# A hybrid decoder layer: the byte positions of the matmul operands in on-chip memory

## Chip, cores, metric

The kernel runs on one core of a Trainium2 chip. The metric is device time in microseconds (us), the median of several executions; lower is better. A profile of one execution comes with it, and "us" and "ns" below are read from that profile or from the times.

## The reference

One decoder layer on 1024 tokens with 16 meta tokens in front (1040 rows of 1024 features), float32. Cut to what matters:

```python
h = concatenate([meta, x])                       # (1040, 1024)
a = rmsnorm(h, ln_mix_pre)
dq, dk, dv, hq, hf, hi, hg = split(a @ w_in)     # w_in: (1024, 3584)
y_diff = diff_attention(dq, dk, dv, ...)         # 4 heads, softmax difference
y_hgrn = hgrn2(hq, hf, hi, hg, ...)              # 4 heads, gated linear recurrence
h = h + rmsnorm(concatenate([y_diff, y_hgrn]) @ w_out, ln_mix_post)
a = rmsnorm(h, ln_ffn_pre)
u = causal_conv3(a @ w_ffn_up) + conv_b          # w_ffn_up: (1024, 5632)
y = (gelu(gate_half(u)) * up_half(u)) @ w_ffn_down   # (2816, 1024)
return (h + rmsnorm(y, ln_ffn_post))[16:]
```

## The kernel before

Nearly all of the time goes into matrix products. A float32 operand is split into a rounded high part and a low part, and a product is made of three matmuls into one PSUM bank: high x high, high x low, low x high. A matmul has a *stationary* operand (128 x 128, loaded into the array by a separate weight load) and a *moving* operand (128 partitions x N columns, streamed through). Each matmul of the program has its own weight load, which the page lists as PEld.

The stages, in the order of the program:

- **Projections**, mixed with attention and recurrence by `interleave` (a generator that feeds projection matmuls between the steps of the heads). Stationary: 128 x 128 pieces of the projection weights (`wh`, `wl`). Moving: the normed activations `ahi`, `alo`, cut in three groups of columns, 272 in the first and 384 in the two others. Lines 237, 239, 241 and 889. With 28 weight tiles, 8 steps of the contraction and three matmuls each, there are 672 matmuls with 272 columns and 1344 with 384. The attention scores are lines 654 and 655.
- **Output projection** in two halves: stationary is the mixed activations (`mp`, from DRAM), moving the split weights, 512 columns. Lines 1016, 1018, 1020.
- **Up stage** of the feed-forward part. The tokens stand in two parts, p = 0 (2 x 258 columns) and p = 1 (2 x 256). For the first of the 22 pairs of feature blocks the products are plain (`plain_unit`, lines 1360 to 1362); for the other 21 each 2 x 2 block product is done with 7 products in the place of 8 (`unit`, lines 1379 to 1381, with `pa`, `pb`, `pc` as the PSUM banks). Stationary: `uh`, `ul`, made from sums of weight tiles. Moving: the activations' sums, tiles `t0_0` to `t0_7` and `t1_0` to `t1_7`, first digit p, second the product; each holds a high and a low half of 4 steps x 258 or 256 columns. They are made by `t_split` and `t_sums` through `t_tiles`, in pools that had room when they were made (`ep`, `mxp`, `tp`, `t2p`).
- **Down stage**, again 7 products in the place of 8: stationary `gh`, `gl`, moving `wh`, `wl`, 512 columns. Lines 1538 to 1540.

TensorE runs in the order in which the code is written. Tiles come from pools: a pool at the left side of the 224 KiB partition grows upwards, a pool at the right side grows downwards, and each tile's byte position follows from the sizes of those allocated before it (rounded up to 32 bytes). Nothing else sets the positions. Worked out from the sizes, as bytes past a multiple of 512: before the change the weights `wh`, `wl`, `uh`, `ul`, the down stage's operands, `mp` and all the p = 1 tiles begin at 480. The p = 0 tiles begin at 480 too, save `t0_0` (352) and `t0_4` (416); their rows are 1032 bytes long, so each of the 4 steps begins 8 bytes later, and most low halves begin 32 bytes after the high ones. `ahi` and `alo` are read at 416 (272 columns) and 480 (384 columns). Every one of the weight positions is thus 32 bytes past a multiple of 64.

Of the kernel before, what the change touches and what calls it, by code (L numbers as in the profile page):

```python
# [9 lines left out]
F32 = mybir.dt.float32  # L10
F32R = mybir.dt.float32r
# [6 lines left out]
P = 128  # L18
# [13 lines left out]
WN = [258, 256]  # L32
# [53 lines left out]
def layer_kernel(ctx: ExitStack, tc: tile.TileContext, x, meta, table, lbl, gpre, gpost, win,  # L86
# [7 lines left out]
    def pool(name, bufs, side="left", space=None):  # L94
        kw = {"side": side} if space is None else {"space": space}
        cm = tc.tile_pool(name=name, bufs=bufs, reuse_waits="tile", **kw)
        return cm, cm.__enter__()

    def close(*cms):
        for cm in cms:  # L100
            cm.__exit__(None, None, None)
# [2 lines left out]
    ctx.enter_context(tc.manual_schedule(engines={mybir.EngineType.PE}))  # L104

    c_cm, cp = pool("const", 1)
    w_cm, wp = pool("weights", 1, "right")
    d_cm, dp = pool("scratch", 1, space=bass.MemoryType.DRAM)
    p_cm, pp = pool("ps0", 1, space=PSUM)
    deep = {"ip": 3, "m": 5}  # L110

    def const(shape, name, dt=F32):
        return cp.tile(shape, dt, tag=name, name=name)
# [12 lines left out]
    nlam = const([P, 1], "nlam")  # L126
    cwt = const([P, 2 * NF, 3], "cwt")
    cbt = const([P, 2 * NF], "cbt")
    m0 = const([P, 88], "m0", F32R)[:, :46]
    G.memset(m0.bitcast(F32), 0.0)  # L130
    m0_7 = const([P, 2, 1, 2], "m0_7", F32R)

# [34 lines left out]
    mx_cm, mxp = pool("mix", 1)  # L167

    MIX = {"X0": 2048, "X1": 2176, "X2": 2176}
# [14 lines left out]
                         m[:, l, off:off + P * n].bitcast(F32).rearrange("p (b c) -> p b c", c=P))  # L184

    at_cm, atp = pool("at", 1)
    ahi, alo = (atp.tile([P, KD, P * NBLK], F32R, tag=t, name=t)[:, :, P - META:] for t in ("ahi", "alo"))

    last_load, lows = [], []
# [771 lines left out]
    p_cm, pp = pool("ps", 2, space=PSUM)  # L961
# [46 lines left out]
    def tok(i):  # L1008
        return (2, 14) if i == 0 else (P, start(i))
# [12 lines left out]
    def meta_part(py, wo, full):  # L1022
        for k in range(KD - 1):
            hi, lo = wo[k]
            both = [(34, hi), (2, lo)]
            if k == KD - 2:
                both.reverse()
            for i, (r, w) in enumerate(both):
                T.matmul(py[:r], m0[:, 2 * k:2 * k + r], w, start=(k == 0 and i == 0), stop=(r == 34 and k == KD - 2))
                yield 216  # L1030
            if k == 0 and full:
                yield from out_part(m0_7, py, wo[KD - 1:], range(1), False, False)
# [18 lines left out]
    def second_load(i):  # L1051
        blocks[i] = block_tile(1, i)
        block_load(blocks[i], i, 0, 4)
        block_load(blocks[i], i, 4, 7 if i == 1 else 8)
# [8 lines left out]
    def y0_gain(p):  # L1063
        r = tok(p)[0]
        return G.tensor_tensor(y0[:r, p], y0[:r, p], gpo0[:r], op=ALU.mult)
# [38 lines left out]
    p_cm, pp = pool("ps3", 8, space=PSUM)  # L1104

    def ps_b(name):
        return pp.tile([P, 512], F32, tag="b", name=name)


    sw_cm, swp = pool("sums", 1, "right")  # L1110
    e_cm, ep = pool("early", 1, "right")
# [74 lines left out]
    def load_xh(i):  # L1186
        r = tok(i)[0]
        if i:
            xhs[i] = qp.tile([P, D], F32, tag="xh", name=f"xh{i}")
        else:  # L1190
            xhs[i], xhs["sum"] = xh0[:, :D], xh0[:, D:]
        SY.dma_start(xhs[i][:r], meta[14:16, :] if i == 0 else x[P * (i - 1): P * i, :])
# [32 lines left out]
    def trans(i):  # L1225
        r, t0 = tok(i)
        a2 = a2t.pop(i)
        cs = slice(t0 - 14, t0 - 14 + r)
        for half in range(2):
            pt = ps_b(f"pa2_{i}_{half}")  # L1230
            for j in range(4):
                k = 4 * half + j
                T.transpose(pt[:, j * r:(j + 1) * r], a2[:r, P * k: P * (k + 1)], ident[:r, :r])
            pv = pt[:, : 4 * r].rearrange("p (k t) -> p k t", k=4)
            ks = slice(4 * half, 4 * half + 4)
            for p in range(2):
                lo_, hi_ = max(cs.start, C0[p]), min(cs.stop, C0[p] + 2 * WN[p])
                if lo_ < hi_:
                    A.copy(
                        at2[p][:, ks, lo_ - C0[p]:hi_ - C0[p]], pv[:, :, lo_ - cs.start:hi_ - cs.start])  # L1240
# [1 line left out]
    tt = [[None] * 8 for _ in range(2)]  # L1242

    def t_tiles(p, j, where, tag):
        tag, n, lo = (tag + (8 * WN[p], 4 * WN[p])[len(tag) - 1:])[:3]
        flat = where.tile([P, n], F32R, tag=tag, name=f"t{p}_{j}")
        return [flat[:, o:o + 4 * WN[p]].rearrange("p (a c) -> p a c", a=4) for o in (0, lo)]

    def t_split(p, j, src, where, *tag):
        hi, lo = t_tiles(p, j, where, tag)  # L1250
        A.copy(hi, src)
        V.tensor_tensor(lo, src, hi.bitcast(F32), op=ALU.subtract)
        tt[p][j] = (hi, lo)

    def quarter(p, j):
        n = WN[p]
        a, c = {0: (0, 0), 7: (0, n), 4: (4, 0), 6: (4, n)}[j]
        return at2[p][:, a:a + 4, c:c + n]

    def t_sums(p, where, last):  # L1260
        b11, b12, b21, b22 = (quarter(p, j) for j in (0, 7, 4, 6))
        V.tensor_tensor(b11, b12, b11, op=ALU.subtract)
        V.tensor_tensor(b12, b22, b12, op=ALU.subtract)
        V.tensor_tensor(b22, b22, b11, op=ALU.subtract)
        for j, b in ((1, b22), (2, b11), (3, b12)):
            t_split(p, j, b, where, f"t{p}_{j}", *(() if p else (2304, 1152) if j == 3 else (2176,)))
        V.tensor_tensor(b21, b21, b22, op=ALU.subtract)
        t_split(p, 5, b21, *last)

    def run(*args):  # L1270
        for _ in out_part(*args):
            pass

    def k7(i):
        return m7[:, i - 1:i].rearrange("p b l t -> p l b t")

    for i in range(1, NBLK):
        py = ps_b(f"py1_{i}")
        if i >= 3:
            y0_gain(i)  # L1280
        if i == 1:
            load_xh(1)
            load_xh(0)
        if i + 1 < NBLK:
            second_load(i + 1)
            load_xh(i + 1)
        run(blocks[i], py, wo, range(4), True, False)
        if i == 3:
            trans(1)
        run(blocks[i], py, wo, range(4, 7 if i == 1 else 8), False, i > 1)  # L1290
        if i > 3:
            trans(i - 2)
        if i == 5:
            trans(0)
        if i == 1:
            pm = ps_b("py1_0")
            for _ in meta_part(pm, wo, True):
                pass
            for p in range(3):
                out_last(p)  # L1300
            run(k7(1), py, wo[KD - 1:], range(1), False, True)
            post(1, py)
            ysum = xhs.pop("sum")
            for l in range(2):
                A.copy(ysum[:2, 512 * l:512 * l + 512], pm[32 * l:32 * l + 2])
            G.tensor_tensor(ysum[:2, :512], ysum[:2, :512], ysum[:2, 512:], op=ALU.add)
            for p in (3, 4):
                out_last(p)
            continue
        post(i, py)  # L1310
        if i == 2:
            post(0, ysum[:, :512], ysum[:, 512:])
        if i == 5:
            t_split(0, 0, quarter(0, 0), ep, "e0")
            t_split(0, 4, quarter(0, 4), ep, "e1")
        if i == 7:
            t_split(0, 7, quarter(0, 7), mxp, "X2", MIX["X2"])
            t_split(0, 6, quarter(0, 6), mxp, "X1", MIX["X1"])
        if i in (2, 3):
            for p in (1 + 2 * i, 2 + 2 * i):  # L1320
                out_last(p)
# [1 line left out]

    xu_cm, xup = pool("xu", 2)
    t_cm, tp = pool("tsplit", 1)
    tp.tile([P, 48], F32, tag="gap", name="gap")

    marks = {}

# [79 lines left out]
    p0 = plain_unit(0, ps_b)  # L1409
    next(p0)  # L1410
    trans(7)
    t_split(1, 0, quarter(1, 0), tp, "t1_0")
    t_split(1, 4, quarter(1, 4), tp, "t1_4")
    for _ in range(3):
        next(p0)
    trans(8)
    t_split(1, 7, quarter(1, 7), tp, "t1_5")
    t_split(1, 6, quarter(1, 6), mxp, "X0")
    t_sums(0, tp, (mxp, "X2", MIX["X2"]))
    close(a_cms.pop())  # L1420
    t2_cm, t2p = pool("tsplit2", 1)
    p1 = plain_unit(1, ps_b)
    for j in range(4):
        prep(7 + j)
        next(p1)
    t_sums(1, t2p, (tp, "t1_5"))
    close(a_cms.pop(), b_cm)
    v_cm, cv = pool("conv", 2, "right")
    cv.tile([P, 56], F32, tag="gap2", name="gap2", bufs=1)
    dn_cm, dn = pool("down", 4, "right")  # L1430
    next(p0)
    for j in range(4, 7):
# [71 lines left out]
    f_cm, fp = pool("fin", 1)  # L1504
# [115 lines left out]
    for m in range(4):  # L1620
        for i in range(len(steps) - TAIL, len(steps)):
            mms(i, m)
        evac(4, m, banks[4][m])
    close(f_cm, dn_cm, v_cm, e_cm, sw_cm, p_cm, d_cm, w_cm, c_cm)


_NAMES = ["x", "meta", "table", "lbl", "gpre", "gpost", "win", "lamv", "subln", "gnorm", "wout",
# [62 lines left out]
```

## Time and profile before

| | |
|---|---|
| median of 3 runs | 1307.94 us (1307.34 to 1311.84) |
| the profiled execution's own time | 1310.98 us |
| its span, first to last instruction | 1309.2 us |
| TensorE busy (PE) | 1275.9 us, 97% |
| weight loads (PEld) | 1186.7 us, 91% |
| VectorE (DVE), ScalarE (ACT), GpSimd (POOL) busy | 68%, 53%, 37% |
| mean granted TensorE clock | 0.996 |

How to read it: matmuls overlap in the array, so the duration that a group of matmuls shows (282 ns for one with 256 columns) is longer than the time from its start to the next one's start. What a matmul costs in a row of them is the distance of the starts, called its *pace* below; it is read from the timeline, or from the number of matmuls in a stretch. Rows of the timeline have the start, the duration, the engine, the line, and what is written and read.

### The profile page before, as it was taken

The page shows a single profiled execution, that of the slowest core. Times are in us where ns is not written, and L with a number is a line of the kernel's source. Part 1 is how long each engine was busy: PE and PEld are TensorE (multiplying, and loading weights), DVE is VectorE, ACT ScalarE, POOL GpSimd, SP SyncE. Part 2 cuts the span into 40 slices and gives each one's busy share as a digit, 9 for nine tenths or more (in the row PEclk, how much of TensorE's full clock was granted, in tenths as well). Part 3 has the DMA queues.
Part 4 walks back from the last instruction along what each step waited for, and adds up shares of the span by engine and source line. Part 5 has one row for each costly group of instructions (what it writes and reads, how often), then busy time and mean ns, then how long its engine had stood idle before and what let it go on. Part 6 is the DMA issues. An engine that isn't in the chain of part 4 may idle for free.

```text
span 1309.2 us, 26099 instructions
## 1 busy us (share of the span) xinstructions
PE 1275.9 (97%) x10154; PEld 1186.7 (91%) x10154; DVE 887.3 (68%) x1488; ACT 697.0 (53%) x1639; POOL 480.8 (37%) x387
## 2 busy tenths in 40 slices
PE   8999999999999999999999999999999999999996
PEld 7999999899999998777999999999999997888885
DVE  7574647465645564457897877778777767797586
ACT  8565466546644754356754544544445434554553
POOL 5231423232313310352066576665665631010121
PEclk9999999999999999999999999999999999999999
DMA  5244655283643533787322222222222127965363
GB/s 213 94 101 86 127 113 113 63 151 81 115 125 68 121 85 102 237 267 257 113 73 74 89 74 81 77 77 90 74 74 89 65 63 266 344 213 169 89 209 121
DMA packets 116418, 165.04 MB, mean 126 GB/s; under 512 B 10099, under 2 KB 57523, under 8 KB 116294
## 3 DMA queue, kind: packets, MB, share of 16 engines
q1 hardware_dynamic: 93062, 151.84, 35.9%
q0 software_dynamic: 23232, 11.54, 7.6%
q8 instruction: 80, 1.31, 0.4%
q14 instruction: 44, 0.36, 0.1%
HBM read 134.24 MB, written 52.17 MB: 142 GB/s over the span
## 4 chain that ended last, share of the span: by engine, by line
PE 82%; DVE 6%; ACT 4%; DMA 4%; issue 2%; SPq 0%; POOL 0%; DVEq 0%; ACTq 0%
PE pd L1539 5%; PE pd L1540 5%; PE pd L1538 5%; PE pb L1379 5%; PE pb L1380 4%; PE pb L1381 4%; PE pa L735 3%; PE pa L1379 3%; PE pa L1381 3%; PE pa L1380 3%; PE pc L1379 3%; PE pc L1380 3%; PE pc L1381 3%; PE pt L711 1%; PE S L655 1%
## 5 line engine op out<-in xcount | busy, mean ns | idle before, releaser
L1379 PE MATMUL pb<-t,uh 128*128 128x258 f32 x504 | 142.8, 283 | 2.3 <-DVE u L53 2.3
L1380 PE MATMUL pb<-t,uh 128*128 128x258 f32 x504 | 142.2, 282 | 0.0
L1381 PE MATMUL pb<-t,ul 128*128 128x258 f32 x504 | 142.1, 282 | 0.0
L1539 PE MATMUL pd<-wl,gh 128*128 128x512 f32 x308 | 120.4, 391 | 2.0 <-DVE wl L53 1.9
L1540 PE MATMUL pd<-wh,gl 128*128 128x512 f32 x308 | 120.0, 390 | 0.0
L1538 PE MATMUL pd<-wh,gh 128*128 128x512 f32 x308 | 120.0, 390 | 0.0
L53 DVE SCALAR_TENSOR_TENSOR c<-uu,cwt,c 128x514 f32<-128x514 f32 (+1 forms) x88 | 97.1, 1103 | 19.6 <-ACT c L53 18.9
L53 POOL TENSOR_TENSOR c<-c,c 128x514 f32<-128x514 f32 (+1 forms) x44 | 63.8, 1450 | 122.6 <-ACT c L53 119.2
L1379 PEld LDWEIGHTS pb<-t,uh 128*128 128x128 f32 x504 | 95.6, 190 | 2.7 <-DVE u L53 2.7
L1380 PEld LDWEIGHTS pb<-t,uh 128*128 128x128 f32 x504 | 96.0, 191 | 0.0
L1381 PEld LDWEIGHTS pb<-t,ul 128*128 128x128 f32 x504 | 95.7, 190 | 0.0
L1379 PE MATMUL pa<-t,uh 128*128 128x258 f32 (+1 forms) x336 | 95.3, 284 | 0.0
L1379 PE MATMUL pc<-t,uh 128*128 128x258 f32 (+1 forms) x336 | 95.1, 283 | 0.0
L1380 PE MATMUL pa<-t,uh 128*128 128x258 f32 (+1 forms) x336 | 95.1, 283 | 0.0
L1380 PE MATMUL pc<-t,uh 128*128 128x258 f32 (+1 forms) x336 | 94.9, 282 | 0.0
L1381 PE MATMUL pa<-t,ul 128*128 128x258 f32 (+1 forms) x336 | 94.8, 282 | 0.0
L1381 PE MATMUL pc<-t,ul 128*128 128x258 f32 (+1 forms) x336 | 94.7, 282 | 0.0
L53 DVE SCALAR_TENSOR_TENSOR c<-ug,cwt,c 128x514 f32<-128x514 f32 (+1 forms) x88 | 88.3, 1004 | 1.6 <-ACT c L53 0.8
L53 ACT CAST uh<-ra 128x512 fp32r<-128x512 f32 x67 | 41.1, 617 | 63.5 <-PE pb L1380 41.8
L53 POOL TENSOR_TENSOR ul<-ws,uh 128x512 fp32r<-128x512 f32 x42 | 59.7, 1421 | 40.4 <-ACT uh L53 40.4
L53 DVE TENSOR_TENSOR ul<-ra,uh 128x512 fp32r<-128x512 f32 x42 | 39.6, 944 | 49.2 <-ACT uh L53 49.2
L1539 PEld LDWEIGHTS pd<-wl,gh 128*128 128x128 f32 x308 | 57.8, 188 | 15.6 <-DVE wl L53 3.6
(388 smaller groups left out, 4170.0 us busy)
## 6 DMA issues: line engine op xcount, KB each, us to landing
ra<-in_wup_dram SPq DMA_DIRECT2D x88, 256.0 KB, 2.9
mp<-msc SPq DMA_DIRECT2D x23, 512.0 KB, 5.6
tsc<-in_wdown_dram SPq DMA_DIRECT2D x44, 256.0 KB, 5.0
wi<-tsc SPq DMA_DIRECT2D x44, 256.0 KB, 2.9
gi<-gsc SPq DMA_DIRECT2D x33, 256.0 KB, 4.7
wi<-in_wdown_dram SPq DMA_DIRECT2D x33, 256.0 KB, 5.3
gsc<-c SPq DMA_DIRECT2D x22, 257.0 KB, 2.1
tsc<-in_wdown_dram POOLq DMA_DIRECT2D x22, 256.0 KB, 7.1
```

The source lines that it names most:

```text
L53: ins = call(*args, **kw)
L655: T.matmul(dst, qs[m][:, q0:q0 + P], kl[m][:, c0:c0 + n], start=False, stop=True)
L711: T.transpose(pt[:b, jj * r:(jj + 1) * r], pb[:r, 0, start(j):start(j) + b], ident[:r, :r])
L735: T.matmul(po[:, :P], w_, vn[:, j], start=(j == 0), stop=(j == i))
L1379: T.matmul(pt, hi[:, s], th[:, k], start=(first and k == 0), stop=False, skip_group_check=True)
L1380: T.matmul(pt, hi[:, s], tl[:, k], start=False, stop=False, skip_group_check=True)
L1381: T.matmul(pt, lo[:, s], th[:, k], start=False, stop=(k == 3), skip_group_check=True)
L1538: T.matmul(py, gh[:, s], wh, start=(k == 0 and pr not in (3, 7)), stop=False, skip_group_check=True)
L1539: T.matmul(py, gh[:, s], wl, start=False, stop=False, skip_group_check=True)
L1540: T.matmul(py, gl[:, s], wh, start=False, stop=(k == NH - 1), skip_group_check=True)
```

## The change

No instruction is added, removed or moved: in the built program each engine has the same instructions with the same waits in the same order before and after, and only tiles' byte positions differ. An unused tile of 480 bytes (`gap0`) is put at the far right, an unused one of 64 bytes (`gap1`) ahead of `ahi`, `m0` is made 32 bytes longer, and `t_tiles` and the calls of `gap` set the distances between the up stage's tiles.

```diff
+    r_cm, rp = pool("edge", 1, "right")
+    rp.tile([P, 120], F32, tag="gap0", name="gap0")
...
-    m0 = const([P, 88], "m0", F32R)[:, :46]
+    m0 = const([P, 96], "m0", F32R)[:, :46]
...
     at_cm, atp = pool("at", 1)
+    atp.tile([P, 16], F32, tag="gap1", name="gap1")
...
     def t_tiles(p, j, where, tag):
-        tag, n, lo = (tag + (8 * WN[p], 4 * WN[p])[len(tag) - 1:])[:3]
-        flat = where.tile([P, n], F32R, tag=tag, name=f"t{p}_{j}")
-        return [flat[:, o:o + 4 * WN[p]].rearrange("p (a c) -> p a c", a=4) for o in (0, lo)]
+        tag, n, off = (tag + (8 * WN[p], 0)[len(tag) - 1:])[:3]
+        both = where.tile([P, n], F32R, tag=tag, name=f"t{p}_{j}")[:, off:off + 8 * WN[p]].rearrange("p (a c) -> p a c", a=8)
+        return both[:, 0:4], both[:, 4:8]
+
+    def gap(where, name, n):
+        where.tile([P, n // 4], F32, tag=name, name=name)
...
         for j, b in ((1, b22), (2, b11), (3, b12)):
-            t_split(p, j, b, where, f"t{p}_{j}", *(() if p else (2304, 1152) if j == 3 else (2176,)))
+            if p and j > 1:
+                gap(where, f"gap5{j}", 64)
+            t_split(p, j, b, where, f"t{p}_{j}")
...
-            t_split(0, 7, quarter(0, 7), mxp, "X2", MIX["X2"])
+            t_split(0, 7, quarter(0, 7), mxp, "X2", MIX["X2"], 16)
...
-    tp.tile([P, 48], F32, tag="gap", name="gap")
...
+    gap(tp, "gap2", 384)
     t_split(1, 0, quarter(1, 0), tp, "t1_0")
+    gap(tp, "gap3", 384)
     t_split(1, 4, quarter(1, 4), tp, "t1_4")
...
+    gap(tp, "gap4", 64)
     t_split(1, 7, quarter(1, 7), tp, "t1_5")
     t_split(1, 6, quarter(1, 6), mxp, "X0")
-    t_sums(0, tp, (mxp, "X2", MIX["X2"]))
+    t_sums(0, tp, (mxp, "X2", MIX["X2"], 16))
```

Worked out in the same way, in bytes past a multiple of 512 after the change:

| operand | before | after |
|---|---|---|
| weights `wh`, `wl`, `uh`, `ul`; down stage's and output projection's operands | 480 | 0 |
| `ahi`, `alo`: 272 columns / 384 columns | 416 / 480 | 0 / 64 |
| p = 1 tiles, products 0 to 6 | 480 each | 192, 320, 384, 448, 64, 128, 0 |
| p = 0 tiles, products 0 to 6 (first step, high half) | 352, 480, 480, 480, 416, 480, 480 | 384, 128, 192, 256, 448, 64, 0 |

The p = 0 steps still begin 8 bytes after one another, and their low halves 32 bytes after the high ones.

More of the change, by code (lines that the diff above doesn't have):

```diff
@@ L1428, in layer_kernel @@
     v_cm, cv = pool("conv", 2, "right")
-    cv.tile([P, 56], F32, tag="gap2", name="gap2", bufs=1)
+    cv.tile([P, 56], F32, tag="gap6", name="gap6", bufs=1)
     dn_cm, dn = pool("down", 4, "right")
@@ L1623, in layer_kernel @@
         evac(4, m, banks[4][m])
-    close(f_cm, dn_cm, v_cm, e_cm, sw_cm, p_cm, d_cm, w_cm, c_cm)
+    close(f_cm, dn_cm, v_cm, e_cm, sw_cm, p_cm, d_cm, w_cm, r_cm, c_cm)
 _NAMES = ["x", "meta", "table", "lbl", "gpre", "gpost", "win", "lamv", "subln", "gnorm", "wout",
```

## The prediction

> **What bounds the kernel now.** I read the page first: the engines' shares, the chain that ended last, the costliest groups.
>
> ```profile
> span 1309.2 us, 26099 instructions
> PE 1275.9 (97%) x10154; PEld 1186.7 (91%) x10154; DVE 887.3 (68%) x1488; ACT 697.0 (53%) x1639; POOL 480.8 (37%) x387
> PE 82%; DVE 6%; ACT 4%; DMA 4%; issue 2%; SPq 0%; POOL 0%; DVEq 0%; ACTq 0%
> L1379 PE MATMUL pb<-t,uh 128*128 128x258 f32 x504 | 142.8, 283 | 2.3 <-DVE u L53 2.3
> L1379 PE MATMUL pa<-t,uh 128*128 128x258 f32 (+1 forms) x336 | 95.3, 284 | 0.0
> L1379 PE MATMUL pc<-t,uh 128*128 128x258 f32 (+1 forms) x336 | 95.1, 283 | 0.0
> L1538 PE MATMUL pd<-wh,gh 128*128 128x512 f32 x308 | 120.0, 390 | 0.0
> ```
>
> TensorE is busy for 97% of the span and carries 82% of the chain. It stands idle for 1309.2 - 1275.9 = 33.3 us only, so a shorter matmul is a shorter kernel, nearly one for one, and a longer one too. Next come stretches (columns: busy time and count of PE, PEld, DVE, ACT, POOL, then the granted clock, the DMA share and GB/s): two of the up stage and the start of the down stage.
>
> ```profile
> 800.00:900.00 100.00, 100.00 (x836) 100.00 (x835) 75.29 (x111) 47.84 (x85) 63.60 (x46) 1.00 0.24 80
> 900.00:1000.00 100.00, 100.00 (x836) 100.00 (x835) 76.45 (x110) 47.09 (x85) 62.28 (x45) 1.00 0.25 80
> 1100.00:1150.00 50.00, 50.00 (x220) 40.78 (x219) 35.02 (x55) 26.55 (x48) 0.54 (x1) 1.00 0.96 336
> ```
>
> In the up stage no other engine is busy for more than 76% and TensorE never pauses at a full clock: about 120 ns per matmul whatever the other engines do. Only at the start of the down stage is something else near its limit: the DMA share is 0.96.
>
> The question is then what a matmul costs from start to start, its pace. The timeline (start, duration, engine, line) gives it in rows where nothing is waited for: 256 columns, then 258, 384, 512 and 272.
>
> ```profile
> 710.72 0.28 PE L1379 MATMUL pc<-t,uh 128*128 128x256 f32 x1
> ...
> 712.16 0.28 PE L1379 MATMUL pb<-t,uh 128*128 128x258 f32 x1
> ...
> 713.60 0.28 PE L1379 MATMUL pb<-t,uh 128*128 128x256 f32 x1
> ```
>
> ```profile
> 127.80 0.33 PE L239 MATMUL pi_hg<-alo,wh_hg 128*128 128x384 f32 x1
> ...
> 129.88 0.33 PE L239 MATMUL pi_hg<-alo,wh_hg 128*128 128x384 f32 x1
> ```
>
> ```profile
> 1120.06 0.39 PE L1540 MATMUL pd<-wh,gl 128*128 128x512 f32 x1
> ...
> 1121.42 0.39 PE L1540 MATMUL pd<-wh,gl 128*128 128x512 f32 x1
> ```
>
> ```profile
> 119.82 0.28 PE L239 MATMUL pi_hg<-alo,wh_hg 128*128 128x272 f32 x1
> ...
> 120.44 0.60 PE L711 MATMUL pt<-ident,pb 128*128 128x128 f32 x4
> ```
>
> A product is 4 steps of three matmuls, so 12 lie between the first two rows and 12 between the second and the third: 1.44/12 = 120 ns for 256 columns and 1.44/12 = 120 ns for 258. The others: 2.08/12 = 173.3 ns for 384, 1.36/6 = 226.7 ns for 512, 0.62/5 = 124 ns for 272. Between 256 and 512 columns lie 106.7 ns, so a column costs 0.417 ns, and 384 columns fit (120 + 128 x 0.417 = 173.3). At that rate 256 columns are 106.7 ns, and **every one of these matmuls is 13.3 ns longer than its columns** (12.5 at 258, 10.7 at 272). That excess is what a change of addresses could take away. In 64-byte pieces, 16 columns or 6.67 ns each, it is exactly two.
>
> **The change part by part.** No instruction and no wait changes, so there are no added or removed operations to cost; all of the effect is in what the operands' positions do to a duration.
>
> *Matmuls with 256, 384 and 512 columns.* Their rows are whole numbers of 64 bytes long, and before the change they begin 32 bytes past a multiple of 64. If an operand is read in whole 64-byte pieces, a row of 256 columns touches 17 in the place of 16, and aligned it saves one piece, 6.67 ns, half of the excess; this holds for 384 and 512 too. The trace has no such row at a multiple of 64, so the price is bounded from both sides: the whole excess (13.3 ns) at the one end and nothing at the other. I take the one piece, because the excess is a whole number of pieces at all three lengths.
>
> The counts: 3 x 308 = 924 in the down stage (the row of L1538 above), 357 with a full 128 rows in the output projection (three lines of the form below), 1344 with 384 columns, and half of 3 x (504 + 336 + 336) = 3528 up-stage matmuls, 1764, with 96 more of the plain product.
>
> ```profile
> L1020 PE MATMUL py<-woh,mp 128*128 128x512 f32 x119 | 47.6, 400 | 0.0
> ```
>
> - 512 columns: 1281 x 6.67 = 8.5 us
> - 384 columns: 1344 x 6.67 = 9.0 us
> - 256 columns: 1860 x 6.67 = 12.4 us
>
> *258 columns* (1860 too): 1032 bytes touch 17 pieces at each of the positions, before and after: nothing. *272 columns* (672): from 18 pieces to 17; the measured 124 ns is already below 18 pieces and the same excess piece, so I take 4 ns, to 120: 2.7 us.
>
> The sum is 32.6 us. A tenth is given back, 3.3 us: the 33.3 us in which TensorE waits stay, the start of the down stage has DMA engines 96% busy and can't follow there, and in the projections the attention steps sit between the matmuls. What is late next is shown by the waits, where the largest entries are 2 us in all:
>
> ```profile
> PE pb L1379 <- DVE u L53: 2.3, 2, 1.4
> PE pg L824 <- DMA grow<-in_gpre_dram: 2.2, 1, 2.2
> PE pt L711 <- DVE at L53: 2.1, 3, 1.0
> ```
>
> In the up stage DVE would be busy for 78 of 100 us in the place of 76, POOL for 65 in the place of 63: they stay covered. The profiled execution took 1310.98 us, 3 us above the median. 1310.98 - 29.3 = 1281.7 for it, and 1307.94 - 29.3 = **1278.6 us** for the median of the runs.
>
> *Here a rule speaks against the change.* The trace can't separate an operand's pieces from a fixed cost of each matmul. The Trainium skill, SBUF — State Buffer, "SBUF: two separate sides" and the note on cachelines under "Door 1", has TensorE on ports of its own that wait for no one, and lines of 16 bytes; 480 is a multiple of 16, so by that page the new positions gain nothing and the sum is 0. On the other hand, TensorE: Matmul & The Clock Gate, "Wait — 56ns, not 53.3ns?", also of the Trainium skill, puts the fixed cost at about 2.5 ns beyond the columns; the 13.3 ns of the rows above are not that, and about 11 ns of them would be open to gain by it (an estimate from that page).
>
> *Operands of the other engines* move by 32 bytes too, and the transfers land elsewhere. No group shows a dependence of theirs on that, and they are covered by TensorE in all stages; I take nothing.
>
> **The rivals.**
>
> *All of the excess goes* because what costs it is that weight and activation rows meet at the same position of 512 (480 and 480), or both are off. How far can it fall? The next weights must be loaded by then. With 128 columns the moving operand needs half of the time, and the load alone sets the pace: 18 such matmuls take 2.01 us in the chain in order of time, 111.7 ns each.
>
> ```profile
> 123.68 2.01 PE pa L735 x18
> ```
>
> So 256 and 258 columns fall by 8.3 ns, 3720 x 8.3 = 30.9 us; 384 and 512 by something between that and the full 13.3, say 10.8, 2625 x 10.8 = 28.4 us; 272 by 8.3, 5.6 us. Together 64.9, less a tenth 58.4: 1250 us. For it: equal positions are the one thing that all of the slow rows share. Against it: the p = 0 tiles stand at many positions against the weights already, and their 120 ns are the same.
>
> *Nothing changes*, 1308 us: the 13.3 ns are a fixed cost of swapping weights. For it: the same figure at three lengths, the 258 columns that don't care for the position, and the 111.7 ns above, where weights at 480 of 512 are loaded with no more than that. Against it: 272 columns, with 10.7.
>
> *It becomes slower*, because equal positions are the good ones. The attention scores have their operands at unequal positions (moving 480 and 224, stationary 352), and with 512 columns their pace is worse:
>
> ```profile
> 229.58 0.40 PE L654 MATMUL E<-k,q 128*128 128x512 f32 x1
> 229.81 0.40 PE L655 MATMUL E<-kl,q 128*128 128x512 f32 x1
> 230.05 0.34 PE L237 MATMUL pi_hi<-ahi,wh_hi 128*128 128x384 f32 x1
> ```
>
> 0.47/2 = 235 ns against 226.7, a piece more. After the change, six of the seven p = 1 tiles and the 384-column rows of `ahi` and `alo` stand 64 or more bytes from the weights' position. If each of those 1584 and 1344 matmuls costs a piece more, that is 2928 x 6.67 = 19.5 us: 1327 us. It decides from the point where the loss at unequal positions is larger than the gain of whole pieces. If both hold, they cancel there, and only the 512 columns of the down stage and output projection gain: 1308 - 8.5 = 1299 us. Against it: 258 columns at unequal positions cost the same 120 ns as 256 at equal ones.
>
> **How the numbers follow.** My forecast, one piece less, has 0.42, all of the excess 0.22, no change 0.15, slower 0.21. A measurement of this kernel can tell about 0.5% from no change, 6.5 us. Faster by more than that is the forecast and the larger gain, 0.64; within it 0.15; slower 0.21. The range reaches down to the larger gain and 10 us below it, 1240, as the weight load's bound is soft, and up to 1316, into the slower case, whose price may be less than the whole piece; what lies above it, and below 1240, is no more than 2 in 10.
>
> **What would show it.** In the changed kernel's timeline, 12 matmuls of 256 columns should take 1.36 us and not 1.44, six of 512 1.32 and not 1.36, 12 of 384 2.00 and not 2.08, while 12 of 258 stay at 1.44; a stretch of 100 us in the up stage should hold about 860 matmuls and not 836. If 258 columns fall as well, it wasn't the pieces but the meeting of the two operands. If p = 1 products differ from one another in pace, their position against the weights counts. Unchanged paces, or 1.52 us for 12 of 256, would make the prediction wrong.

## The result, and the profile after

The changed kernel takes **1303.25 us** (median of 6 runs, 1302.75 to 1305.37); the kernel before, timed beside it, 1308.3 us (6 runs, 1307.34 to 1311.84). The ratio is 0.9958, 95% interval 0.9944 to 0.9972. About 5 us were gained where 29.3 were forecast: inside the half per cent called "no change", and inside the range.

The page of the changed kernel: the span, the engines, and two groups that answer to those of before.

```profile
span 1303.5 us, 26099 instructions
PE 1271.0 (98%) x10154; PEld 1182.5 (91%) x10154; DVE 885.6 (68%) x1488; ACT 695.8 (53%) x1639; POOL 482.6 (37%) x387
L1386 PE MATMUL pb<-t,uh 128*128 128x258 f32 x504 | 142.2, 282 | 2.7 <-DVE u L53 2.6
L1548 PE MATMUL pd<-wh,gh 128*128 128x512 f32 x308 | 120.0, 390 | 0.0
```

The span is 5.7 us shorter (1309.2 - 1303.5) and TensorE's busy time 4.9 us less; no other engine comes near it. The down stage's group has the same 120.0 us. The same two stretches of the up stage as before, in the windows view (PE, PEld, DVE, ACT, POOL, clock, DMA share, GB/s):

```profile
800.00:900.00 100.00, 99.99 (x844) 99.78 (x843) 76.18 (x112) 48.47 (x86) 64.73 (x46) 1.00 0.22 78
900.00:1000.00 100.00, 100.00 (x846) 100.00 (x845) 76.13 (x111) 48.07 (x85) 63.78 (x46) 1.00 0.25 85
```

844 and 846 matmuls are in 100 us where 836 were; 860 were forecast. Within the up stage the products are no longer alike. In the timeline of one pair of feature blocks, these are first matmuls of products (12 matmuls each). The order is product 0 with p = 0 (258 columns), product 0 with p = 1 (256 columns), product 1 with p = 0, and so on.

```profile
843.38 0.28 PE L1386 MATMUL pa<-t,uh 128*128 128x256 f32 x1
...
844.75 0.29 PE L1386 MATMUL pb<-t,uh 128*128 128x258 f32 x1
...
846.20 0.28 PE L1386 MATMUL pb<-t,uh 128*128 128x256 f32 x1
...
847.61 0.28 PE L1386 MATMUL pc<-t,uh 128*128 128x258 f32 x1
...
851.92 0.28 PE L1386 MATMUL pb<-t,uh 128*128 128x256 f32 x1
...
853.29 0.28 PE L1386 MATMUL pa<-t,uh 128*128 128x258 f32 x1
```

`t1_0` takes 844.75 - 843.38 = 1.37 us, 114 ns per matmul; `t1_1` 1.41 us, 117.5 ns; `t1_3` 1.37 us. Before, 12 such matmuls took 1.42 to 1.44 us. The whole up stage, from its first matmul to the first of the down stage, in the timeline of before and of after:

```profile
660.42 0.28 PE L1379 MATMUL pa<-t,uh 128*128 128x258 f32 x1
...
1086.19 0.40 PE L1538 MATMUL pd<-wh,gh 128*128 128x512 f32 x1
```

```profile
658.98 0.28 PE L1386 MATMUL pa<-t,uh 128*128 128x258 f32 x1
...
1080.97 0.40 PE L1548 MATMUL pd<-wh,gh 128*128 128x512 f32 x1
```

It shrinks from 425.8 to 422.0 us, 3.8 of the span's 5.7 us. The 384 and 512 columns of the stretches shown before, again 12 and 6 matmuls apart in the changed kernel's timeline:

```profile
127.83 0.34 PE L242 MATMUL pi_hg<-alo,wh_hg 128*128 128x384 f32 x1
...
129.91 0.34 PE L242 MATMUL pi_hg<-alo,wh_hg 128*128 128x384 f32 x1
...
1119.92 0.39 PE L1550 MATMUL pd<-wh,gl 128*128 128x512 f32 x1
...
1121.28 0.39 PE L1550 MATMUL pd<-wh,gl 128*128 128x512 f32 x1
```

2.08 and 1.36 us, as before: the 64-byte boundary gained nothing in these stretches. (Over the whole execution the mean distance of the 384 columns did fall, see below.)

### The profile page after: what moved, and what is told of

Read it like the earlier page. It is cut to its first block, busy times and chain, and to the rows that moved or that the text cites. A ratio compares the mean times of both kernels' runs of the same rounds, so it can differ in the third digit from the quotient of the medians.

```text
span 1303.5 us, 26099 instructions
## 1 busy us (share of the span) xinstructions
PE 1271.0 (98%) x10154; PEld 1182.5 (91%) x10154; DVE 885.6 (68%) x1488; ACT 695.8 (53%) x1639; POOL 482.6 (37%) x387
## 4 chain that ended last, share of the span: by engine, by line
PE 46%; DVE 4%; ACT 2%; issue 1%; DMA 1%; DVEq 0%; ACTq 0%
PE pd L1549 5%; PE pd L1550 5%; PE pd L1548 5%; PE pb L1386 5%; PE pb L1387 4%; PE pb L1388 4%; PE pa L1386 3%; PE pa L1388 3%; PE pc L1386 3%; PE pa L1387 3%; PE pc L1388 3%; PE pc L1387 3%; DVE t L53 1%; DVE xh L53 1%; DVE c L53 1%
## 5 line engine op out<-in xcount | busy, mean ns | idle before, releaser
L1550 PE MATMUL pd<-wh,gl 128*128 128x512 f32 x308 | 120.1, 390 | 0.0
L53 POOL TENSOR_TENSOR c<-c,c 128x514 f32<-128x514 f32 (+1 forms) x44 | 63.8, 1449 | 122.4 <-ACT c L53 120.3
```

The source lines that it names most:

```text
L53: ins = call(*args, **kw)
L1550: T.matmul(py, gl[:, s], wh, start=False, stop=(k == NH - 1), skip_group_check=True)
```

## The experiments

All paces below are mean distances between the starts of neighbouring matmuls of one kind, over the whole profiled execution (about 250 for each tile of the up stage, about 540 for 272 columns, 900 to 1000 for 384 and 512, without the few distances in which something was waited for). *Position* is the moving operand's byte address less the weights', modulo 512. The theory after the result: it is this position that counts, not the 64-byte boundary. The rival: the boundary, with something that hid its gain.

**e1_zero**: the boundary alone. Everything begins at multiples of 64, but all p = 1 tiles stand at the weights' position, as they did before.

```diff
-    gap(tp, "gap2", 384)
+    gap(tp, "gap2", 192)
...
-    gap(tp, "gap3", 384)
...
-    gap(tp, "gap4", 64)
...
-            if p and j > 1:
-                gap(where, f"gap5{j}", 64)
+            if p and j == 1:
+                gap(where, "gap5", 320)
```

> The changed kernel, but all seven p = 1 tiles of the up stage stand at 0 past the weights' position (both at byte 0 of 512), so they are aligned to 64 bytes and stand at the weights' position. If aligned rows are what helped (whole pieces), the 256-column matmuls keep the 117.1 ns mean pace of the changed kernel or fall to 113.3, and the time stays at about 1303 us. If the position against the weights is what counts, they go back to about 119.4 to 120 ns as before the change, 1764 x 2.3 to 2.9 ns = 4 to 5 us slower than the changed kernel, about 1307.5 us. 258 columns: 120 either way.

1306.82 us, ratio to before 0.9989 (0.9977 to 1.0002): no change. 256 columns take 119.28 ns against 119.38 before. The windows row of 800 to 900 us, and `t1_1` in the timeline:

```profile
800.00:900.00 100.00, 100.00 (x838) 100.00 (x837) 75.45 (x111) 47.70 (x86) 63.65 (x46) 1.00 0.23 80
```

```profile
843.24 0.28 PE L1386 MATMUL pb<-t,uh 128*128 128x256 f32 x1
...
844.67 0.28 PE L1386 MATMUL pc<-t,uh 128*128 128x258 f32 x1
```

838 matmuls and 1.43 us. The step of the prediction that saves a piece by alignment has fallen.

**e2_old192**: the position alone. This is the kernel before, with its weights at 480; products 0 to 5 of p = 1 are put at 160, which is 192 past 480 modulo 512 and no multiple of 64. Product 6 stays.

```diff
-    tp.tile([P, 48], F32, tag="gap", name="gap")
+    tp.tile([P, 96], F32, tag="gap", name="gap")
...
-            t_split(p, j, b, where, f"t{p}_{j}", *(() if p else (2304, 1152) if j == 3 else (2176,)))
+            t_split(p, j, b, where, f"t{p}_{j}", *(() if p else (2176,)))
```

> The kernel before, nothing aligned to 64 bytes, weights at 480 of 512; only p = 1 tiles 0 to 5 are moved to 160 of 512, 192 past the weights (and the p = 0 tiles 1 to 3 with them). Tile t1_6 stays at the weights' position as a control. If the position against the weights alone counts, tiles 0 to 5 fall from 119.4 to about 113.5 ns, the pace that t1_0 has at 192 in the changed kernel, t1_6 stays at 119.4 to 120, and the time is 1512 x 5.9 ns = 8.9 us below before, about 1299 us. If it needs rows at multiples of 64 as well, they stay at 118 to 120 ns and the time at about 1308 us.

1303.49 us, ratio 0.9959 (0.9944 to 0.9974): all of the change's gain without its boundary. `t1_0` and `t1_1` in the timeline:

```profile
841.17 0.28 PE L1379 MATMUL pa<-t,uh 128*128 128x256 f32 x1
...
842.53 0.28 PE L1379 MATMUL pb<-t,uh 128*128 128x258 f32 x1
...
843.96 0.28 PE L1379 MATMUL pb<-t,uh 128*128 128x256 f32 x1
...
845.38 0.28 PE L1379 MATMUL pc<-t,uh 128*128 128x258 f32 x1
```

1.36 and 1.42 us, at the same position. So the position counts, but it isn't all: of the six products at 192, two took 113.3 to 113.6 ns and four 117.7 to 118.0.

**e3_six192**: the changed kernel with products 0 to 5 of p = 1 at 192 or 448.

```diff
-    gap(tp, "gap3", 384)
...
-    gap(tp, "gap4", 64)
...
-            if p and j > 1:
-                gap(where, f"gap5{j}", 64)
+            if p and j == 1:
+                gap(where, "gap5", 64)
```

> The changed kernel with p = 1 tiles 0 to 5 all at 192 or 448 past the weights (192 past a multiple of 256), the two positions that were fastest there (113.6 and 114.6 ns); t1_6 stays at 0. By the position theory all six run at 113.5 to 114.5 ns, against a mean of 116.9 now: 1512 x 2.9 ns = 4.4 us below the changed kernel, about 1299 us. If those two tiles were fast for another reason (their place in the partition, or the product that comes before them), only t1_0 and t1_3 stay fast, and the time is about 1303 us.

1302.86 us, ratio 0.9952 (0.9939 to 0.9966). Four of the six ran at 113.3 to 113.9 ns, two (`t1_1`, `t1_4`) at 118.0. `t1_1` and `t1_2`, both at 448:

```profile
844.73 0.28 PE L1386 MATMUL pb<-t,uh 128*128 128x256 f32 x1
...
846.14 0.28 PE L1386 MATMUL pc<-t,uh 128*128 128x258 f32 x1
...
847.56 0.28 PE L1386 MATMUL pc<-t,uh 128*128 128x256 f32 x1
...
848.92 0.28 PE L1386 MATMUL pb<-t,uh 128*128 128x258 f32 x1
```

In e2 and e3 together every slow product follows a p = 0 product that itself stands at 192 or 448, and no fast one does. That gave the next theory: a product's pace is set by its position *and by the rhythm in which it is entered*.

**e4_ends192**: other lengths at 192. The up stage is that of the changed kernel; 384 columns move from 64 to 192, 272 columns from 0 to 128, the down stage's 512 columns from 0 to 192.

```diff
-    atp.tile([P, 16], F32, tag="gap1", name="gap1")
+    atp.tile([P, 48], F32, tag="gap1", name="gap1")
...
-    cv.tile([P, 56], F32, tag="gap6", name="gap6", bufs=1)
+    cv.tile([P, 104], F32, tag="gap6", name="gap6", bufs=1)
```

> The changed kernel with the two long forms at other positions against their weights: 384 columns 192 past them (64 in the changed kernel), 272 columns 128 past (0), and 512 columns of the down stage 192 past their stationary operand (0). If 192 past is good whatever the length, 384 falls from 173.4 to about 166.7 ns and 512 from 226.8 to about 220 ns: 9.0 + 6.2 = 15 us, about 1288 us. If the attention scores are the better guide (512 columns at 128 past: 233 ns), the down stage gets 6 us slower and the time is about 1309 us. No effect on either if only 256 columns, whose length is just that of the next weight load, react.

1310.65 us, ratio 1.0014 (1.0001 to 1.0026), 7.4 us above the changed kernel. Six matmuls of the down stage in the timeline:

```profile
1119.54 0.40 PE L1550 MATMUL pd<-wh,gl 128*128 128x512 f32 x1
...
1120.94 0.40 PE L1550 MATMUL pd<-wh,gl 128*128 128x512 f32 x1
```

1.40/6 = 233.3 ns against 226.7: for 512 columns the equal position is better than 192, and 924 x 6.6 ns = 6.1 us is most of the loss. What helps one length harms another.

**e5_entry** and **e6_swap**: the entry. Both have products 0 to 5 of p = 1 at 192 or 448, and move the p = 0 tiles that run ahead of them. The edit of e5 against e3; e6 has 128 for `gap8` and keeps `gap5` with 192:

```diff
             t_split(0, 4, quarter(0, 4), ep, "e1")
+            ep.tile([P, 16], F32, tag="gap7", name="gap7")
...
+    gap(tp, "gap8", 64)
     t_sums(0, tp, (mxp, "X2", MIX["X2"], 16))
...
-            if p and j == 1:
-                gap(where, "gap5", 64)
...
-    cv.tile([P, 56], F32, tag="gap6", name="gap6", bufs=1)
+    cv.tile([P, 40], F32, tag="gap6", name="gap6", bufs=1)
```

> Like e3_six192 (products 0 to 5 of p = 1 at 192 past the weights' position, modulo 256), but the p = 0 tiles that run just before products 1 and 4 are moved off that place: t0_1, t0_2, t0_3 from 192, 256, 320 to 256, 320, 384, t0_0 and t0_4 from 384 and 448 to 320 and 384. Theory (the pace of a 256-column product is set by its position and by how it is entered: it stays near 118 ns where the product ahead of it stands at 192 modulo 256, near 113.4 elsewhere): t1_1 and t1_4 fall from 118.0 to 113.4 ns, the other four stay at 113.4, so 504 matmuls x 4.6 ns = 2.3 us less than e3_six192, about 1300.5 us. Rival (the slow ones are slow by their tile, bank or absolute address): t1_1 and t1_4 stay at 118, 1302.9 us. Rival (the paces fall into one of two values by chance): some other product is slow in their place.

> The same, but t0_1, t0_2, t0_3 at 320, 384, 448, and t1_1 to t1_3 at 192. Only product 3 now follows a p = 0 product that stands at 192 modulo 256. Entry theory: t1_3 rises from 113.9 (in e3_six192) to 118 ns, while t1_1 and t1_4 are at 113.4. Tile rival: t1_1 and t1_4 are the slow ones, t1_3 stays near 113.9.

e5: 1301.4 us, ratio 0.9942 (0.9929 to 0.9956); e6: 1301.18 us in one run. In e5 `t1_1` and `t1_4` fell to 113.3 and 114.6 ns as expected, and in e6 `t1_3`, now entered from 448, rose to 117.4 while `t1_1` was at 113.3. But in both `t1_0` had become slow, 117.8 ns, behind a `t0_0` at 320, a position from which `t1_3` (in e3) and `t1_2` (in e5) were entered at 113.9 and 113.3. So a rule on the preceding tile's position alone is wrong as well. `t1_0` and `t1_1` of e5, and then `t1_3` of e6:

```profile
840.91 0.28 PE L1385 MATMUL pa<-t,uh 128*128 128x256 f32 x1
...
842.33 0.28 PE L1385 MATMUL pb<-t,uh 128*128 128x258 f32 x1
...
843.75 0.28 PE L1385 MATMUL pb<-t,uh 128*128 128x256 f32 x1
...
845.11 0.28 PE L1385 MATMUL pc<-t,uh 128*128 128x258 f32 x1
```

```profile
847.76 0.28 PE L1387 MATMUL pb<-t,uh 128*128 128x256 f32 x1
...
849.17 0.28 PE L1387 MATMUL pa<-t,uh 128*128 128x258 f32 x1
```

At the positions 0 and 192 the weight loads show a difference too. The groups of PEld (behind the bar: busy us, then the mean ns of one load) within three products: `t1_1` of before once it has settled, `t1_1` of e5, `t1_0` of e5.

```profile
L1380 PEld LDWEIGHTS pb<-t,uh 128*128 128x128 f32 x3 | 0.6, 192 | 0.0
```

```profile
L1386 PEld LDWEIGHTS pb<-t,uh 128*128 128x128 f32 x4 | 0.8, 188 | 0.0
```

```profile
L1387 PEld LDWEIGHTS pa<-t,ul 128*128 128x128 f32 x4 | 0.8, 192 | 0.0
L1386 PEld LDWEIGHTS pa<-t,uh 128*128 128x128 f32 x4 | 0.8, 188 | 0.0
```

At 0 and at 192 (modulo 256) a product settles in a steady rhythm, and stays in it to its end. There are three: every load 188 ns and every matmul 113.3; one load in three 192 and the matmuls 117.7 on average; every load 192 and every matmul 120. At 192 it is one of the first two, at 0 the products of all these kernels come to the third. In before, `t1_1`, `t1_2`, `t1_5` and `t1_6` begin with one matmul of 113 or 114 ns and are in the third rhythm from the third on, in the pair of feature blocks from 844.5 us on, to which the first group above belongs.

Elsewhere neither the three rhythms nor the sign of the loads hold. In the changed kernel `t1_1`, at 320, ran steadily at 117.5 ns with no load of 192, and inside `t1_2`, at 384, the distances of the starts go from 113 to 124 ns and don't settle. And the down stage's loads take 188 ns at 226.8 ns per matmul (changed kernel) and at 233.3 (e4). The loads of `t1_1` in the changed kernel, then those of the down stage from 1110 to 1140 us, in the changed kernel and in e4:

```profile
L1388 PEld LDWEIGHTS pb<-t,ul 128*128 128x128 f32 x4 | 0.8, 188 | 0.0
L1387 PEld LDWEIGHTS pb<-t,uh 128*128 128x128 f32 x3 | 0.6, 188 | 0.0
```

```profile
L1548 PEld LDWEIGHTS pd<-wh,gh 128*128 128x128 f32 x44 | 8.3, 188 | 1.7
```

```profile
L1548 PEld LDWEIGHTS pd<-wh,gh 128*128 128x128 f32 x43 | 8.1, 188 | 1.9
```

**e9_seven**: whether the rhythm is carried over. Product 6 of p = 1 goes to 192 too; all others keep their places modulo 256 (the weights now at 256).

```diff
-    rp.tile([P, 120], F32, tag="gap0", name="gap0")
+    rp.tile([P, 56], F32, tag="gap0", name="gap0")
...
-    MIX = {"X0": 2048, "X1": 2176, "X2": 2176}
+    MIX = {"X0": 2096, "X1": 2176, "X2": 2176}
...
-    t_split(1, 6, quarter(1, 6), mxp, "X0")
+    t_split(1, 6, quarter(1, 6), mxp, "X0", MIX["X0"], 48)
```

(and `gap1`, `gap2` and a new gap of 64 bytes ahead of `woh`, so that the rest keeps its place modulo 256)

> Like e5_entry, with product 6 of p = 1 (t1_6, until now at 0) also at 192 modulo 256 past the weights' position; all other operands keep their places modulo 256 (the weights now at 256 of 512). Theory of the entry: t1_6 falls from 118.8 to 113.4 ns, and with it t1_0, which follows after it and t0_0, and which e5_entry showed at 117.8 because t1_6 left the matmuls in the slow rhythm: to 113.4 as well. 252 x (5.4 + 4.4) = 2.5 us less than e5_entry, 1299 us. If only a tile's own place counts: t1_6 at 113.4, t1_0 still at 117.8: 1.4 us less. If t0_0 at 320 sets the pace of t1_0, the same.

`t1_6` fell from 118.8 to 114.3 ns, and `t1_0` from 117.8 to 113.3 with its own position and `t0_0`'s unchanged modulo 256. Between e5 and e9 the pace of `t1_0` was thus set by the product two ahead of it. That product alone is no rule either: in e3 `t1_0` ran at 113.6 ns behind a `t1_6` of 118.8, with `t0_0` at 384. The time is 1301.17 us, ratio 0.9943 (0.9928 to 0.9958), not the 1299 that was worked out: 0.2 us less than e5, within the error. Two things took the gain. `t0_1`, entered from the faster `t1_0`, now runs in a worse rhythm, 122.4 ns and not 118.2, and all p = 0 products together rise from 119.95 to 120.70: of the 1764 x 1.19 = 2.1 us that p = 1 wins, 1764 x 0.75 = 1.3 are given back. Product 0 with p = 1, product 1 with p = 0, and product 6 with p = 1 in the timeline:

```profile
840.03 0.28 PE L1386 MATMUL pa<-t,uh 128*128 128x256 f32 x1
...
841.39 0.28 PE L1386 MATMUL pb<-t,uh 128*128 128x258 f32 x1
...
842.86 0.28 PE L1386 MATMUL pb<-t,uh 128*128 128x256 f32 x1
...
856.93 0.28 PE L1386 MATMUL pc<-t,uh 128*128 128x256 f32 x1
...
858.31 0.28 PE L1386 MATMUL pa<-t,uh 128*128 128x258 f32 x1
```

1.36, 1.47 and 1.38 us. The second taker is a wait. Product 3 is added into the bank `pb` that product 1 has filled, and it starts only when VectorE has read that bank (`u<-pb,x`). In the first pairs TensorE waits 3.1 us for this in e5 and 3.2 in e9. From 720 to 1080 us the weight loads wait for it too: 0.2 us in all in the changed kernel, 1.2 in e5 and 1.9 in e9, where it happens about every 40 us. One such pause in e9 (two operations of VectorE in a row, and the load that was held up), and the waits in e5 and e9:

```profile
727.55 0.74 DVE L53 TENSOR_TENSOR u<-pb,x 128x258 f32<-128x258 f32 x2
...
728.02 0.19 PEld L1386 LDWEIGHTS pb<-t,uh 128*128 128x128 f32 x1 [0.23 <-DVE u L53]
```

```profile
PEld pb L1385 <- DVE u L53: 1.2, 7, 0.2
```

```profile
PEld pb L1386 <- DVE u L53: 1.9, 8, 0.3
```

All distances above 140 ns in the up stage exceed 120 ns by 2.9 us together in before, 3.6 in after, 5.0 in e3, 5.7 in e5 and 6.5 in e9.

**e7_scan** and **e8_ends64**: other positions. e7 is the changed kernel with its gaps set otherwise; e8 is e5 with `gap1` of 32 bytes in the place of 64, and `gap6` 64 bytes longer.

```diff
-    gap(tp, "gap2", 384)
...
-    gap(tp, "gap3", 384)
+    gap(tp, "gap3", 32)
...
-            if p and j > 1:
-                gap(where, f"gap5{j}", 64)
+            if p:
+                gap(where, f"gap5{j}", 32 * j)
...
+    gap(tp, "gap8", 96)
...
-    atp.tile([P, 16], F32, tag="gap1", name="gap1")
+    atp.tile([P, 32], F32, tag="gap1", name="gap1")
...
-    cv.tile([P, 56], F32, tag="gap6", name="gap6", bufs=1)
+    cv.tile([P, 120], F32, tag="gap6", name="gap6", bufs=1)
```

> The changed kernel with the positions spread over others: p = 1 products 0 to 6 at 320, 224, 288, 384, 352, 416, 0; 384-column rows at 128 and 272-column rows at 64 past the weights' position; the down stage's moving operand at 256. Theory (the effect depends on the distance modulo 256 and is smooth around 192): 256 columns near 192 (224, 416) are faster than at 288 and 352, which are near 119; the down stage is at 227 ns again as at 0, because 256 is the same place; 384 columns between 173.4 and 174.5 ns. Rival with a period of 512: the down stage is slower than 227 ns, up to the 233 of e4_ends192. Rival that only multiples of 64 can be fast: 224, 288, 352 and 416 all at 119 to 120 ns.

> Like e5_entry, with the down stage's moving operand at 64 (0 before) and the 384-column rows at 32, the 272-column rows at 480 past the weights' position (64 and 0 before). Theory (each length has its own good and bad places; a pace falls below 13.3 ns over its columns only where the weight loads don't meet the moving reads): the 512 columns were at 226.9 ns at 0 and 256 and at 233.3 at 192; at 64 they stay at 226.9 if the bad places are few, fall to 220.0 (one 64-byte piece less, as 256 columns fell to 113.3) if 64 is their good place, or are near 233 if 0 is the only good one. 384 columns at 32 lie between 174.8 (at 0) and 173.4 (at 64). Rival (512 columns are bound by something else, the position only adds): never below 226.7.

e7: 1309.5 us, e8: 1305.02 us, one run each; what follows rests on the paces. Six matmuls of the down stage at 256 (e7), then at 64 (e8):

```profile
1120.00 0.39 PE L1550 MATMUL pd<-wh,gl 128*128 128x512 f32 x1
...
1121.36 0.39 PE L1550 MATMUL pd<-wh,gl 128*128 128x512 f32 x1
```

```profile
1119.67 0.39 PE L1548 MATMUL pd<-wh,gl 128*128 128x512 f32 x1
...
1121.04 0.39 PE L1548 MATMUL pd<-wh,gl 128*128 128x512 f32 x1
```

1.36 us at 256, as at 0, which fits a pattern that repeats after 256 bytes (as do the fast products at 192 and at 448); 1.37 at 64. No position brought 512 columns below 226.8 ns. For 256 columns my smooth picture around 192 is wrong: 224 and 416 took 117.8 and 118.4 ns, hardly better than 352 (119.5), and 288, farther off, took 116.9. And 384 columns at 128 were slower than I expected. The mean paces in ns by position:

| position | 0 (256) | 32 | 64 | 128 | 192 |
|---|---|---|---|---|---|
| 512 columns, down stage | 226.9 (226.9) | | 228.9 | | 233.3 |
| 384 columns | 174.8 | 174.4 | 173.4 | 175.9 | 174.5 |
| 256 columns, p = 1 (modulo 256) | 118.4 to 120.1 | 116.9 | 117.6 to 118.3 | 118.1 to 119.0 | 113.3 to 114.9, or 117.4 to 118.0 |
| 272 columns (modulo 256) | 125.2 to 125.3 | | 125.9 | 126.3 | 123.8 |

The 272 columns stood at 448, which is 192 modulo 256, before the change: the best of their places that were run. The change moved them to 0. Two executions with 384 columns at the same place, before and e2, differ by 0.2 ns (174.8 and 175.0); so much is scatter, and 174.4 to 174.8 can't be told apart.

And the up stage, mean paces in ns (e4 has that of the changed kernel, e8 that of e5, and e7 took 118.24). Before, timed beside each group of runs, had medians from 1307.92 to 1309.06 us; the table has the one beside the changed kernel.

| | before | after | e1 | e2 | e3 | e5 | e6 | e9 |
|---|---|---|---|---|---|---|---|---|
| p = 1, 256 columns | 119.38 | 117.10 | 119.28 | 116.76 | 115.59 | 115.15 | 115.61 | 113.96 |
| median of the runs, us | 1308.3 | 1303.25 | 1306.82 | 1303.49 | 1302.86 | 1301.4 | 1301.18 | 1301.17 |

## Why the prediction was wrong, point by point

- *TensorE bounds the kernel, and a shorter matmul is a shorter kernel.* Right. The changes of pace add up to 1764 x 2.28 + 1764 x 0.30 + 96 x 2.2 + 1344 x 1.38 - 672 x 1.36 = 5.7 us (256 and 258 columns, the plain product, 384, 272), and the span fell by 5.7 us. That the two agree to the tenth is luck: in the up stage the paces give 4.8 us, waits take 0.7 back and 3.8 were found; outside it the paces give 0.9 and 1.9 were found. DVE and POOL, at 77% and 65% of the up stage's stretches at most, stayed covered but for waits on DVE that grew by some tenths of a us.
- *Excess 13.3 ns, exactly two 64-byte pieces.* The reading was right, and the best rhythm at 256 columns, 113.3 ns, is one such piece less to the digit. But the numbers' fit was no evidence for its cause.
- *"If an operand is read in whole 64-byte pieces, a row of 256 columns touches 17 in the place of 16, and aligned it saves one piece."* **This is the step that failed.** e1_zero aligns the up stage's p = 1 rows and the down stage's and gains nothing there; e2_old192 gains all without aligning. The terms that hung on it: 512 columns 8.5 us forecast, 0.1 found in the down stage (226.94 to 226.83, and 226.92 in e1_zero) and nothing in the output projection (228.4 both times); 384 columns 9.0 forecast, 1.9 found, and e4 and e7, with rows at multiples of 64 bytes, have 174.5 and 175.9 ns against the 174.8 of before, so that length varies with the position; 256 columns 12.4 forecast, 4.2 found, by position; 272 columns 2.7 forecast, 0.9 lost (123.85 to 125.21), by position too, as far as the four places of the table show. An aligned 384-column row at position 0 wasn't run, so the part of the boundary in its 1.9 us stays open.
- *258 columns: nothing.* Right in size (120.37 to 120.07). But I used them as evidence that the position is irrelevant ("the p = 0 tiles stand at many positions ... and their 120 ns are the same"). Product by product they ran at 118.2 to 122.4 ns in these runs, and within one product of before (`t0_1`, from 847.39 us on) the distances go from 113 to 125 ns. A mean over a mixture was read as a constant. Their steps drift by 8 bytes, so each product may average over good and bad places; no run tests that.
- *A tenth is given back.* No idle time grew that much in the changed kernel: the waits on `u` went from 2.3 to 2.6 us, and TensorE's idle time in all from 33.3 to 32.5. What a faster down stage would have waited for, one of the reasons given, was not tested, as it became no faster. In the faster variants waits and slower p = 0 products did take some.
- *The rivals.* "No change", with 0.15, holds the result. The mechanism of "all of the excess goes" has one half right for 256 columns, that the position against the weights counts. But equal positions are not what costs: unequal ones of 32, 64, 96, 128, 160 and 224 modulo 256 took 116.9 to 119.5 ns, hardly less than equal ones, and only 192 gave 113.3, which is also above the 111.7 named as the floor. For 512 columns "equal positions are the good ones" fits better: e4 measured 233.3 at 192, and the scores, quoted with 235 from two rows, have a mean of 233.8 in before. The change leaves 512 columns at equal positions, so that loss didn't occur.
- *The rules of the Trainium skill.* SBUF — State Buffer, "SBUF: two separate sides", by which the sum was 0, was nearer to the measured 5 us than my 29.3, and e1_zero, where alignment gained nothing, agrees with it. It has no place for e2_old192 and e5_entry: the same loads and matmuls went from 192 and 120 ns to 188 and 113.3 through addresses alone. TensorE: Matmul & The Clock Gate, "Wait — 56ns, not 53.3ns?", also of the Trainium skill, has 2.5 ns beyond the columns; the least that any stretch here shows is 6.7 ns (113.3 - 106.7).
- *"If p = 1 products differ from one another in pace, their position against the weights counts."* This is what the changed kernel's trace showed.

What stays open: why 192 bytes modulo 256 is the place where 256 columns can run free, and what in TensorE's reading makes a load 188 or 192 ns long. For 256 columns at 0 and 192 the runs show that load, matmul and position go together; they don't show which waits for which, and at other positions and lengths the loads don't follow the pace. What decides the rhythm in which a product is entered is open too: neither the position of the product ahead nor the pace of the one two ahead is a rule by itself.

## What to carry to other kernels

Where TensorE is the bound and each matmul has its own weight load, measure the pace by the distance of starts for each operand tile apart, not for a line: in e9_seven a mean of 117.3 ns over the up stage hides products from 113.3 to 122.4. Move a moving operand relative to its weights (here modulo 256 bytes) before caring for alignment, try it for each length by itself, and leave alone a length that is at its best: 512 columns lost 6.5 ns by the move that gave 256 columns 6. Expect to keep only a part: a faster product enters the next one in another rhythm, and the engine that empties the banks must keep up.

The fastest versions (e5_entry 1301.4, e9_seven 1301.17, e6_swap 1301.18 in a single run) are 1.9 to 2.1 us below the changed kernel by their medians; their ratios' intervals overlap with that of the changed kernel, so the times don't show them to be faster; the paces of the p = 1 products do fall.

## What the runs showed of the hardware that I had not expected

- Float32 matmuls with 256 columns settle at 120 ns at position 0 modulo 256, with weight loads of 192 ns, and at 192 either at 113.3 with loads of 188 or at 117.7 with one load of 192 in three. At other positions the distances can go on changing (113 to 124 ns inside `t1_2` of the changed kernel), and 117.5 ns come without a load of 192 (`t1_1`).
- Which pace it is depends on the moving operand's position against the weights modulo 256 bytes, and, at 192, on the products that ran before it: `t1_0` at the same places took 117.8 ns (e5) or 113.3 (e9) as product 6, two products ahead, ran in one rhythm or the other.
- The good place depends on the length: 512 columns 226.9 ns at 0 and 233.3 at 192; 384 columns 173.4 at 64 and 175.9 at 128; 272 columns 123.8 at 448 and 126.3 at 128; 256 columns 119.3 at 0 and, well entered, 113.3 at 192.
- Addresses at multiples of 64 bytes were no better than addresses 32 bytes off (119.28 against 119.38 ns for 256 columns, 226.83 against 226.94 for 512).
